# Which engine makes the sums of W_down's blocks, and when: sixteen sets moved between attention, mix, W_o and W_up

## The chip, the cores and the metric

The kernel runs on one core of a Trainium2 chip. The metric is the device time of one execution in microseconds (us). Matmuls run on TensorE (PE), elementwise work on VectorE (DVE), ScalarE (ACT) and GpSimd (POOL); SyncE (SP) issues nearly all transfers.

## The reference

One layer on a stream of 512 tokens by 1024 channels, all in fp32:

```python
h = rms_norm(x, g_pre_mix)
q, k, v, cb, cc, cu, ga, gc = split(h @ w_in)           # 5120 columns
y_attn = stick_breaking_attention(q, k, v) @ w_attn_out  # 8 heads of 64
y_conv = (cb * causal_depthwise_conv(cc * cu, w_conv)) @ w_conv_out
m = sigmoid(ga + b) * y_attn + sigmoid(gc + b) * y_conv
x = x + rms_norm(m @ w_o, g_post_mix)
h = rms_norm(x, g_pre_mlp)
f = square(relu(h @ w_up)) @ w_down                      # 4096 wide
x = x + rms_norm(f, g_post_mlp)
x = x + sigmoid(rms_norm(x, g_ple) @ w_ple_gate) * (p @ w_ple_proj)
```

Stick-breaking attention takes the scores z of a head, `beta = sigmoid(z)` and `keep = sigmoid(-z)`, masks both to the strictly causal part, and multiplies beta by the running product of keep from the right.

## The kernel before

Each fp32 operand of a product is split into a high part (a cast on ACT, line L64, tiles `whi`, `wth`, `oyh`) and the rest (a subtraction on DVE, L65, `wlo`, `wtl`, `oyl`), and each product is three matmuls (L89 to L91, helper `mm3`). Weights come in pieces of 512 KB into `raw` tiles (L70, four buffers) and are split there. The stages follow one another: a head that norms and projects v; attention, four rounds j of two heads each, with the conv branch woven in; mix, eight rounds j (the two output projections, gates, product); W_o; W_up; W_down; the gate at the end.

W_up and W_down are computed by a block scheme that needs sums of blocks of the weights (seven products in place of eight). For W_down the sums are made ahead of time. `make_sums` does one of sixteen sets: it saves the set before it (L279, two transfers of 512 KB from tiles `w` to DRAM, `wsum`), loads two pieces of `w_down` (L290, 512 KB each), and makes four sums of 128x512 (L296) on POOL, or on the engine that it is handed. `save_sums` alone issues the transfers to DRAM. Before, two sets are made ahead of attention and four in it (one a round, all on DVE), eight in mix (one a round, on POOL), and two in W_o (k = 0 and 2, on POOL).

What orders the work: PE and SP run in the order in which the code is written (`manual_schedule`). The others are ordered by a scheduler by priority; `tc.high_priority(-LATE)` puts a block 150 places later in that order. Whatever the order, each engine then runs its instructions one after the other, and one that waits holds up all behind it.

In a round of attention, `scores` makes 1280 columns of beta and keep for a head on ACT (L329, L330). POOL masks them (L335, AFFINE_SELECT of 128x128), and DVE runs the products (L338, a scan, four a head, and L339). The conv branch is on DVE too: L385 multiplies by a projection in a PSUM bank, L388 and L390 make the convolution, L395 multiplies by the last projection and so frees its bank. `wtrans` turns beta over on PE (L354) and splits it; `av` multiplies it by v (L368). `proj_q` and `proj_k` lay out the next round's q and k in `st` (L304, L306; L314, whose high parts ACT casts at L313); PE's scores (L326, L327) read them.

Of the kernel before, what the change touches and what calls it, by code (L numbers as in the profile page):

```python
# [25 lines left out]
LATE = 150  # L26
# [7 lines left out]
def hybrid_block(ctx, tc, x, p, g_pre_mix, w_in, b_gate, w_conv, w_attn_out, w_conv_out, w_o,  # L34
                 g_post_mix, g_pre_mlp, w_up, w_down, g_post_mlp, g_ple, w_ple_gate, w_ple_proj, out):
    nc = tc.nc
# [23 lines left out]
    def tm(dt=F32):  # L60
        return tmp.tile([P, 512], dt, tag="tmp", name="tmp")
# [16 lines left out]
    def w4(dt=F32):  # L78
        return wts.tile([P, 2, 512], dt, tag="w", name="w4")
# [196 lines left out]
    def save_sums():  # L276
        while unsaved:
            dst, src = unsaved.pop(0)
            nc.sync.dma_start(dst, src)  # L279
# [3 lines left out]
    def make_sums(eng=None):  # L283
        eng = eng or nc.gpsimd
        save_sums()
        j = next(made)
        q = []
        for h in range(2):
            t = w4()
            nc.sync.dma_start(t, wd[j][h].rearrange("p (c n) -> p c n", c=2))  # L290
            q += [t[:, 0], t[:, 1]]
        dst = wsum[j // 2][:, :, j % 2, :]
        o = [w4(), w4()]
        t1, t2, t3, t4 = (o[i // 2][:, i % 2] for i in range(4))
        for r, x_, y_ in ((t1, q[1], q[0]), (t2, q[3], t1), (t3, q[3], q[1]), (t4, q[2], t2)):
            eng.tensor_tensor(r, x_, y_, op=ALU.subtract)  # L296
        unsaved.extend([(dst[:, 0:2], o[0]), (dst[:, 2:4], o[1])])
# [95 lines left out]
    def conv_b(c, y):  # L393
        ps = proj(wcols(w_in, 1536 + c * P), hx)
        nc.vector.tensor_tensor(y, ps, y, op=ALU.mult)  # L395
        split(oy_h[1][:, c], oy_l[1][:, c], y)
# [15 lines left out]
    for j in range(4):  # L412
        wa = scores(st[0])
        wb = scores(st[1])
        y = conv_u(j, ct)
        conv_b(j, y)
        ta = wtrans(wa)
        if j < 3:
            st = proj_q(j + 1)
        else:  # L420
            sg[0] = gate(0, 0)
        tb = wtrans(wb)
        if j < 3:
            proj_k(j + 1, st)
        else:
            sg[1] = gate(0, 1)
        of = tm()
        with tc.high_priority(-LATE):
            make_sums(nc.vector)
        av(2 * j, ta, of)  # L430
        av(2 * j + 1, tb, of)
        if j < 3:
            ct = conv_c(j + 1)
# [11 lines left out]
    def oyc(part):  # L445
        return lambda k: (oy_h[part][:, k, :], oy_l[part][:, k, :])

    for j in range(NK):
        make_sums()
        sa, sc = sg if j == 0 else (next_gate if j == 1 else gate(j, 0), gate(j, 1))  # L450

        def two(t, j=j):
            return [(t[:, 4 * i:4 * i + 4], w[:, j * P:(j + 1) * P].rearrange("(k p) m -> p k m", p=P))
                    for i, w in ((1, w_conv_out), (0, w_attn_out))]

        wo2 = weights(two, [P, NK, P])
        save_sums()
        py = proj(wo2, oyc(1), 4, 4)
        nc.vector.tensor_tensor(sc, sc, py, op=ALU.mult)
        if j == 0:  # L460
            next_gate = gate(1, 0)
        py = proj(wo2, oyc(0), 4, 0)
        nc.vector.tensor_tensor(sa, sa, py, op=ALU.mult)
        nc.vector.tensor_tensor(sa, sa, sc, op=ALU.add)
        split(m_h[j // 4][:, j % 4], m_l[j // 4][:, j % 4], sa)
        if j == 3:
            for t in range(NT):
                nc.sync.dma_start(xr[t // 2][:, t % 2, :], x[t * P:(t + 1) * P, :])
        if j == 6:
            nc.sync.dma_start(pf, p[0].rearrange("(t p) d -> p t d", p=P))  # L470
            nc.sync.dma_start(wpr, w_pp.rearrange("(k p) m -> p k m", p=P))
            split(wph, wpl, wpr)
        if j == 7:
            for kk in range(2):
                ps = bank()
                for t in range(NT):
                    nc.tensor.transpose(ps[:, t * P:(t + 1) * P], pf[:, t, kk * P:(kk + 1) * P], ident)
                split(pt[:, kk], pt[:, 2 + kk], ps)


    def rows(nk, stat, w, tail, chain):
        acc = {}
        held = {}
        for k in range(nk):
            if k in (0, 2):
                make_sums()
            if k in (1, 3):
                save_sums()
            wk = wrow(w, k)
            if k >= nk - tail:  # L490
                held[k] = wk
                continue
            sh, sl = stat(k)
            for t in range(NT):
                tok = slice(t * P, (t + 1) * P)
                for hf in range(2):
                    if k == 0:
                        acc[t, hf] = bank()
                    cs = slice(hf * 512, (hf + 1) * 512)
                    mm3(acc[t, hf], sh[:, tok], sl[:, tok], wk[0][:, cs], wk[1][:, cs], k == 0, False)  # L500
        for t in range(NT):
            tok = slice(t * P, (t + 1) * P)
            for hf in range(2):
                cs = slice(hf * 512, (hf + 1) * 512)
                for k in range(nk - tail, nk):
                    sh, sl = stat(k)
                    wk = held[k]
                    mm3(acc[t, hf], sh[:, tok], sl[:, tok], wk[0][:, cs], wk[1][:, cs], False, k == nk - 1)
            chain(t, [acc[t, 0], acc[t, 1]])
# [114 lines left out]
    def up_load(c):  # L624
        r = []
        for h in range(2):
            raw = raws.tile([P, NK, P], F32, tag="raw", name="raw")
            nc.sync.dma_start(raw, w_up[:, (c + h * NJ) * P:(c + h * NJ + 1) * P].rearrange("(k p) m -> p k m", p=P))
            r.append(raw)
        a11, a12, a21, a22 = r[0][:, 0:4], r[0][:, 4:8], r[1][:, 0:4], r[1][:, 4:8]  # L630

        def both(n0, n1, src):
            if c == FIRST or n0 == 6:
                hl = bigt([P, 2, NK, P], name="us")
                hi, lo = hl[:, 0], hl[:, 1]
            else:
                lo, hi = (wts.tile([P, NK, P], F32R, tag="w", name="us") for _ in range(2))
            split(hi, lo, src)
            up_s[c, n0] = hi[:, 0:4], lo[:, 0:4]
            up_s[c, n1] = hi[:, 4:8], lo[:, 4:8]  # L640

        s1 = s1p.tile([P, 4, P], F32, tag="s1", name="s1")
        nc.vector.tensor_tensor(s1, a21, a22, op=ALU.add)
        both(1, 2, r[0])
        nc.vector.tensor_tensor(a11, s1, a11, op=ALU.subtract)
        nc.vector.tensor_tensor(a21, a12, a11, op=ALU.subtract)
        nc.vector.tensor_tensor(a12, a22, a11, op=ALU.subtract)  # L647
        both(6, 7, r[0])
        one_ = wts.tile([P, 2, 4, P], F32R, tag="w", name="us1")
        split(one_[:, 0], one_[:, 1], s1)  # L650
        up_s[c, 5] = one_[:, 0], one_[:, 1]
        both(3, 4, r[1])

    def up_mm(c, n):
        onto = n in (6, 5, 3, 4)
        key = {6: 1, 5: 1, 3: 1, 4: 7}.get(n, n)
        if not onto:
            up_ps[c, n] = bank()
        ps = up_ps[c, key][:, 0:256]
        sh, sl = up_s[c, n]  # L660
        th, tl = rt[n]
        for k in range(4):
            mm3(ps, sh[:, k], sl[:, k], th[:, k], tl[:, k], k == 0 and not onto, k == 3, onto)
        if n == 1:
            ct[c] = [tm(), tm()]
            nc.scalar.copy(ct[c][0][:, 0:256], ps)
        c11, c12, c21, c22 = (ct[c][i // 2][:, 256 * (i % 2):256 * (i % 2) + 256] for i in range(4))
        if n == 2:
            nc.vector.tensor_tensor(c11, ps, c11, op=ALU.add)
        elif n == 6:  # L670
            nc.scalar.copy(c21, ps)
        elif n == 7:
            nc.scalar.copy(c22, ps)
        elif n == 5:
            nc.vector.tensor_tensor(c22, ps, c22, op=ALU.add)
        elif n == 4:
            nc.vector.tensor_tensor(c21, ps, c21, op=ALU.add)
        elif n == 3:
            nc.scalar.copy(c12, ps)
            for h in range(2):  # L680
                nc.scalar.activation(ct[c][h], ct[c][h], AF.Relu)
                nc.scalar.activation(af[c // 4 + 4 * h][:, c % 4], ct[c][h], AF.Square)
            if c % 4 == 3:
                g = c // 4
                nc.vector.tensor_tensor(quarter(1, 0, g), quarter(1, 0, g), quarter(1, 1, g), op=ALU.add)
# [8 lines left out]
    for _, c, n in order:  # L694
        if n == 6 and c + 1 < NJ:
            up_load(c + 1)
        up_mm(c, n)


# [188 lines left out]
```

## Time and profile before

| what | value |
|---|---|
| time, median of three runs | 746.45 us (744.97 to 746.55) |
| the profiled execution's own time | 746.06 us |
| its span in the profile | 744.0 us, so 2.06 us lie around it |
| busy: PE, DVE, ACT, POOL | 730.5, 539.1, 396.2, 108.0 us |
| share of the chain that ended last | PE 82%, DVE 6%, DMA 5%, ACT 3%, POOL 2% |

Times within the profile are us from the start of the span. A timeline row gives the start, the length, and in brackets how long the engine had sat idle before it and what ended that. Rows of the same kind that follow each other closely are merged (x3).

### The profile page before, as it was taken

Reading aid. Unit: us, or ns where it says so; the run is one execution under the profiler, and the core shown is the slowest. Engines: PE = TensorE matmul, PEld = TensorE weight load, DVE = VectorE, ACT = ScalarE, POOL = GpSimd, SP = SyncE. Lnnn points to the kernel's source line nnn. Section 1 sums busy time; section 2 is a strip of 40 time slices with the busy share of each in tenths; the row PEclk is TensorE's granted clock in tenths of the full one; section 3 lists DMA queues with packets and bytes.
Section 4 is the critical chain, followed back from the end, with each engine's and each line's share of the span. In section 5 each row is a group of like instructions: output and inputs, shape, how many; then the busy total and the mean of one; then the engine's idle time right before and its main releaser. Section 6 shows DMA issues by size and latency. Waiting matters only on the chain.

```text
span 744.0 us, 10442 instructions
## 1 busy us (share of the span) xinstructions
PE 730.5 (98%) x3936; PEld 632.4 (85%) x3936; DVE 539.1 (72%) x747; ACT 396.2 (53%) x672; POOL 108.0 (15%) x131
## 2 busy tenths in 40 slices
PE   7999999998999999999999999999999999999997
PEld 6888788887888888878899999999988888888876
DVE  4889898959755424554869879977699878268762
ACT  6555656462533322442855776867776476256531
POOL 0005051347425222200100000000000000001100
PEclk8999999999999999999999999999999999999999
DMA  8393727157599885752244444432555767577311
GB/s 310 126 327 107 221 100 227 54 199 252 178 346 273 254 281 193 269 161 57 106 178 112 115 115 114 118 110 86 168 160 174 224 243 230 174 245 263 128 58 58
DMA packets 112107, 132.30 MB, mean 178 GB/s; under 512 B 4116, under 2 KB 82744, under 8 KB 111032
## 3 DMA queue, kind: packets, MB, share of 16 engines
q1 hardware_dynamic: 111480, 127.44, 53.8%
q10 hardware_dynamic: 576, 4.19, 1.4%
q8 instruction: 31, 0.51, 0.3%
q14 instruction: 20, 0.16, 0.1%
HBM read 108.55 MB, written 23.07 MB: 177 GB/s over the span
## 4 chain that ended last, share of the span: by engine, by line
PE 82%; DVE 6%; DMA 5%; ACT 3%; POOL 2%; issue 1%; SPq 1%; DVEq 0%; POOLq 0%; ACTq 0%
PE ps L89 26%; PE ps L90 26%; PE ps L91 26%; DVE wlo L65 1%; DMA w<-in_w_down_dram 1%; DMA raw<-wsum 1%; PE ps L368 1%; POOL w L296 1%; DMA xin<-in_x_dram 1%; DMA wsum<-w 1%; DMA raw<-in_w_o_dram 1%; ACT whi L64 1%; DVE keep L338 1%; PE ps L354 1%; PE ps L548 1%
## 5 line engine op out<-in xcount | busy, mean ns | idle before, releaser
L65 DVE TENSOR_TENSOR wlo<-raw,whi 128x512 fp32r<-128x512 f32 x120 | 89.4, 776 | 45.8 <-ACT whi L64 19.7
L89 PE MATMUL ps<-h1h,whi 128*128 128x512 f32 x288 | 113.8, 395 | 2.7 <-DVE tmp L395 2.7
L91 PE MATMUL ps<-h1h,wlo 128*128 128x512 f32 x288 | 112.8, 392 | 0.0
L90 PE MATMUL ps<-h1l,whi 128*128 128x512 f32 x288 | 112.7, 391 | 0.0
L64 ACT CAST whi<-raw 128x512 fp32r<-128x512 f32 x120 | 69.1, 638 | 49.6 <-DMA raw<-in_w_in_dram 16.0
L89 PE MATMUL ps<-w,sb 128*128 128x512 f32 x216 | 84.1, 389 | 0.0
L91 PE MATMUL ps<-w,sb 128*128 128x512 f32 x216 | 84.0, 389 | 0.0
L90 PE MATMUL ps<-w,sb 128*128 128x512 f32 x216 | 84.0, 389 | 0.0
L65 DVE TENSOR_TENSOR w<-raw,w 128x1024 fp32r<-128x1024 f32 x56 | 67.7, 1222 | 22.0 <-PE ps L90 11.6
L64 ACT CAST w<-raw 128x1024 fp32r<-128x1024 f32 x56 | 58.4, 1051 | 37.5 <-DMA raw<-wsum 13.4
L125 POOL TENSOR_TENSOR rs<-ms,mhalf 128x1 f32<-128x1 f32 x20 | 14.5, 726 | 409.0 <-DVE ms L121 367.6
L89 PEld LDWEIGHTS ps<-h1h,whi 128*128 128x128 f32 x288 | 54.5, 189 | 13.8 <-DVE tmp L395 2.9
L91 PEld LDWEIGHTS ps<-h1h,wlo 128*128 128x128 f32 x288 | 54.3, 189 | 11.5
L90 PEld LDWEIGHTS ps<-h1l,whi 128*128 128x128 f32 x288 | 54.6, 189 | 11.0
L89 PE MATMUL ps<-h2h,us 128*128 128x256 f32 x224 | 63.5, 283 | 0.0
L90 PE MATMUL ps<-h2l,us 128*128 128x256 f32 x224 | 63.4, 283 | 0.0
L91 PE MATMUL ps<-h2h,us 128*128 128x256 f32 x224 | 63.4, 283 | 0.0
L65 DVE TENSOR_TENSOR us<-raw,us 128x1024 fp32r<-128x1024 f32 x42 | 50.7, 1219 | 7.9 <-ACT us L64 7.7
L64 ACT CAST us<-raw 128x1024 fp32r<-128x1024 f32 x42 | 43.4, 1050 | 19.1 <-DVE raw L647 7.5
L89 PE MATMUL ps<-tb,us 128*128 128x256 f32 x168 | 47.9, 285 | 0.0
L90 PEld LDWEIGHTS ps<-w,sb 128*128 128x128 f32 x216 | 40.5, 188 | 8.5
L89 PEld LDWEIGHTS ps<-w,sb 128*128 128x128 f32 x216 | 40.5, 188 | 8.4
(206 smaller groups left out, 1715.6 us busy)
## 6 DMA issues: line engine op xcount, KB each, us to landing
raw<-in_w_in_dram SPq DMA_DIRECT2D x36, 512.0 KB, 6.9
w<-in_w_down_dram SPq DMA_DIRECT2D x32, 512.0 KB, 4.3
wsum<-w SPq DMA_DIRECT2D x32, 512.0 KB, 3.8
raw<-in_w_up_dram SPq DMA_DIRECT2D x32, 512.0 KB, 4.5
raw<-wsum SPq DMA_DIRECT2D x32, 512.0 KB, 5.1
raw<-in_w_down_dram SPq DMA_DIRECT2D x24, 512.0 KB, 4.3
raw<-in_w_o_dram SPq DMA_DIRECT2D x8, 512.0 KB, 6.0
raw<-in_w_ple_gate_dram SPq DMA_DIRECT2D x8, 512.0 KB, 6.7
```

The source lines that it names most:

```text
L64: nc.scalar.copy(hi, src)
L65: nc.vector.tensor_tensor(lo, src, hi.bitcast(F32), op=ALU.subtract)
L89: nc.tensor.matmul(ps, lh, rh, start=start, stop=False, skip_group_check=onto)
L90: nc.tensor.matmul(ps, lh, rl, start=False, stop=False, skip_group_check=onto)
L91: nc.tensor.matmul(ps, ll, rh, start=False, stop=stop, skip_group_check=onto)
L125: nc.gpsimd.tensor_tensor(r, m, mhalf, op=ALU.pow)
L296: eng.tensor_tensor(r, x_, y_, op=ALU.subtract)
L338: nc.vector.tensor_tensor_scan(kr, kr, kr, 1.0, op0=ALU.mult, op1=ALU.bypass)
L354: nc.tensor.transpose(ps[:, c0 + (qb - kb) * P:c0 + (qb - kb + 1) * P], w[:, o:o + P], ident)
L368: nc.tensor.matmul(ps[:, kb * P:S], lhs, wt[i][:, c0:c0 + n], start=(kb == 0 and i == 0), stop=(kb == NT - 1 and i == 1))
L548: nc.tensor.transpose(ps[:, i * P:(i + 1) * P], hn1[t][g][:, i * P:(i + 1) * P], ident)
```

## The change

The sixteen sets stay; what changes is where each is made and on which engine. Attention makes two (rounds 1 and 2, on DVE) in place of four. Mix makes its first two on DVE at the late priority and the other six on POOL. W_o makes three, one on POOL (k = 0) and two on DVE at the ordinary priority (k = 1 and 3). W_up makes the last, on DVE, at the loads of its sixth chunk (c = 4), and saves it at c = 6. So DVE makes nine sets in place of six, and POOL seven in place of ten. No matmul moves.

```diff
@@ attention, round j
-        with tc.high_priority(-LATE):
-            make_sums(nc.vector)
+        if j in (1, 2):
+            with tc.high_priority(-LATE):
+                make_sums(nc.vector)
         av(2 * j, ta, of)
@@ mix
     for j in range(NK):
-        make_sums()
+        if j > 1:
+            make_sums()
+        else:
+            with tc.high_priority(-LATE):
+                make_sums(nc.vector)
@@ W_o (function rows)
-            if k in (0, 2):
-                make_sums()
-            if k in (1, 3):
+            if k in (0, 1, 3):
+                make_sums(nc.gpsimd if k == 0 else nc.vector)
+            if k == 4:
                 save_sums()
@@ W_up
         if n == 6 and c + 1 < NJ:
             up_load(c + 1)
+            if c == 4:
+                make_sums(nc.vector)
+            if c == 6:
+                save_sums()
```

Because the sets are handed out in turn, the first set of mix in the changed kernel takes about the place that attention's fourth had. Lines below attention carry higher numbers in the changed kernel; the tile numbers (`w_848`) differ too.

DVE before the scores of attention's round 0, kernel before (`wlo` rows are weight splits, `st` rows the layout of q and k, the scan is the first of the round):

```order
L306 TENSOR_TENSOR st<-ps,st 64x512
L65 TENSOR_TENSOR wlo<-raw,whi 128x512 x3
L314 TENSOR_TENSOR st<-ps,st 64x512 x2
L296 TENSOR_TENSOR w_848<-w_844 128x512
L314 TENSOR_TENSOR st<-ps,st 64x512
L296 TENSOR_TENSOR w_848<-w_846,w_848 128x512
L314 TENSOR_TENSOR st<-ps,st 64x512
L296 TENSOR_TENSOR w_849<-w_846,w_844 128x512
L296 TENSOR_TENSOR w_849<-w_846,w_848 128x512
L338 SCALAR_TENSOR_TENSOR keep<-keep 128x512
```

The same place in the changed kernel:

```order
L306 TENSOR_TENSOR st<-ps,st 64x512
L65 TENSOR_TENSOR wlo<-raw,whi 128x512 x5
L314 TENSOR_TENSOR st<-ps,st 64x512 x3
L65 TENSOR_TENSOR wlo<-raw,whi 128x512
L314 TENSOR_TENSOR st<-ps,st 64x512
L65 TENSOR_TENSOR wlo<-raw,whi 128x512
L338 SCALAR_TENSOR_TENSOR keep<-keep 128x512
```

Four sums are gone, and the splits of two further weight pieces stand there instead, two splits of them ahead of all the `st` of k.

POOL around the masks of attention's round 3, kernel before (`w_1955` is mix's first set, `w_2042` its second):

```order
L296 TENSOR_TENSOR w_1955<-w_1951 128x512
L296 TENSOR_TENSOR w_1955<-w_1953,w_1955 128x512
L296 TENSOR_TENSOR w_1956<-w_1953,w_1951 128x512
L296 TENSOR_TENSOR w_1956<-w_1953,w_1955 128x512
L335 AFFINE_SELECT beta<-beta 128x128
L335 AFFINE_SELECT keep<-keep 128x128
```

POOL after the last masks of that round in the changed kernel (`w_2105` is mix's third set):

```order
L335 AFFINE_SELECT beta<-beta 128x128
L335 AFFINE_SELECT keep<-keep 128x128
L296 TENSOR_TENSOR w_2105<-w_2101 128x512
L296 TENSOR_TENSOR w_2105<-w_2103,w_2105 128x512
L296 TENSOR_TENSOR w_2106<-w_2103,w_2101 128x512
```

No sum stands ahead of round 3's masks any more; the first that follows them is mix's third set.

DVE in round 3, from the last `st` of k to the first scan, kernel before:

```order
L65 TENSOR_TENSOR oyl<-tmp,oyh 128x512
L314 TENSOR_TENSOR st<-ps,st 64x512
L338 SCALAR_TENSOR_TENSOR keep<-keep 128x512
L339 TENSOR_TENSOR beta<-beta,keep 128x511
```

The same place in the changed kernel, and further on, from L385 to L395 (`w_2018` and `w_2019` are mix's second set):

```order
L314 TENSOR_TENSOR st<-ps,st 64x512
L65 TENSOR_TENSOR wlo<-raw,whi 128x512 x2
L296 TENSOR_TENSOR w_2018<-w_2014 128x512
L338 SCALAR_TENSOR_TENSOR keep<-keep 128x512
...
L385 TENSOR_TENSOR tmp<-tmp,ps 128x512
L296 TENSOR_TENSOR w_2018<-w_2016,w_2018 128x512
L388 TENSOR_SCALAR tmp<-tmp,cols 128x512
L296 TENSOR_TENSOR w_2019<-w_2016,w_2014 128x512
L390 SCALAR_TENSOR_TENSOR tmp<-tmp,cols 128x511
L65 TENSOR_TENSOR wlo<-raw,whi 128x512
L390 SCALAR_TENSOR_TENSOR tmp<-tmp,cols 128x510
L296 TENSOR_TENSOR w_2019<-w_2016,w_2018 128x512
L395 TENSOR_TENSOR tmp<-ps,tmp 128x512
```

One sum, which needs the load of `w_2014`, now stands ahead of round 3's first scan, and three stand among the steps of the convolution.

## Rows read from the trace of the kernel before

**Rows 1.** Waits of PE: us in total, times, longest.

```profile
PE ps L89 <- DVE tmp L395: 2.7, 1, 2.7
...
PE ps L368 <- DVE wtl L65: 0.3, 1, 0.3
PE ps L327 <- DVE st L314: 0.3, 1, 0.3
PE ps L89 <- DVE pt L65: 0.2, 1, 0.2
```

**Rows 2.** Timeline of PE, second turning of beta in attention's round 1.

```profile
111.74 1.25 PE L354 MATMUL ps<-ident,beta 128*128 128x128 f32 x10
112.75 0.48 PE L89 MATMUL ps<-h1h,whi 128*128 128x512 f32 x1
```

**Rows 3.** Timeline of PE, the same step of round 3.

```profile
180.93 1.25 PE L354 MATMUL ps<-ident,beta 128*128 128x128 f32 x10
184.88 0.80 PE L89 MATMUL ps<-h1h,whi 128*128 128x512 f32 x1 [2.71 <-DVE tmp L395]
...
187.98 0.39 PE L90 MATMUL ps<-h1l,whi 128*128 128x512 f32 x1
```

**Rows 4.** Windows: length, engines' busy us, then PEclk, DMA share, GB/s.

```profile
185.00:190.00 5.00, 5.00 (x16) 4.05 (x17) 4.91 (x7) 5.00 (x12) 3.96 (x3) 0.71 0.98 302
```

**Rows 5.** Timeline of POOL in round 3.

```profile
161.03 3.79 POOL L296 TENSOR_TENSOR w<-w,w 128x512 f32<-128x512 f32 x3
...
175.67 4.89 POOL L296 TENSOR_TENSOR w<-w,w 128x512 f32<-128x512 f32 x3
```

**Rows 6.** Timeline of DVE in round 3.

```profile
165.35 1.29 DVE L338 TENSOR_TENSOR_SCAN keep<-keep 128x512 f32<-128x512 f32 x1 [6.21 <-POOL keep L335]
...
177.91 1.50 DVE L339 TENSOR_TENSOR beta<-beta,keep 128x255 f32<-128x255 f32 x1
...
184.14 0.69 DVE L395 TENSOR_TENSOR tmp<-ps,tmp 128x512 f32<-128x512 f32 x1
```

**Rows 7.** Timeline of DVE in round 2, the same steps.

```profile
128.49 1.23 DVE L338 TENSOR_TENSOR_SCAN keep<-keep 128x512 f32<-128x512 f32 x1 [0.92 <-POOL keep L335]
...
139.10 0.41 DVE L339 TENSOR_TENSOR beta<-beta,keep 128x255 f32<-128x255 f32 x1
...
144.27 0.68 DVE L395 TENSOR_TENSOR tmp<-ps,tmp 128x512 f32<-128x512 f32 x1
```

**Rows 8.** Timeline of ACT at the start of round 3.

```profile
161.74 0.62 ACT L64 CAST whi<-raw 128x512 fp32r<-128x512 f32 x1 [3.46 <-DMA raw<-in_w_conv_out_dram]
...
163.35 0.61 ACT L330 ACTIVATE keep<-ps 128x512 f32<-128x512 f32 x1
```

**Rows 9.** The chain that ended last: start, us, what; attention's round 0.

```profile
71.08 5.84 DMA wsum<-w
...
76.97 3.73 DMA w<-in_w_down_dram
...
94.42 0.23 PE ps L89
```

**Rows 10.** Timeline of DVE in round 0.

```profile
80.79 0.69 DVE L296 TENSOR_TENSOR w<-w 128x512 f32<-128x512 f32 x1 [1.52 <-DMA w<-in_w_down_dram]
```

**Rows 11.** Timeline of ACT ahead of round 0's scores.

```profile
44.85 0.62 ACT L64 CAST whi<-raw 128x512 fp32r<-128x512 f32 x1 [0.67 <-DMA raw<-in_w_in_dram]
...
46.66 0.62 ACT L64 CAST whi<-raw 128x512 fp32r<-128x512 f32 x1 [0.18 <-DMA raw<-in_w_in_dram]
```

**Rows 12.** Timeline of PE, second head's scores in round 0.

```profile
56.93 0.40 PE L327 MATMUL ps<-st 128*128 128x512 f32 x1
```

**Rows 13.** Loads of `raw` (line L70) from 36 to 60 us.

```profile
DMA to landing us min/median/max: 5.0/7.0/9.1
```

**Rows 14.** Loads of the blocks of W_down (line L290), the whole span.

```profile
DMA to landing us min/median/max: 3.2/4.3/7.9
```

**Rows 15.** Windows, a stretch of W_up (columns as in rows 4).

```profile
400.00:450.00 50.00, 50.00 (x416) 49.81 (x415) 43.59 (x61) 34.98 (x60) 0.00 (x0) 1.00 0.45 127
```

## The prediction

> **What bounds the kernel now.** I read the waits of PE first, since PE is busy in nearly the whole span: only work that PE waits for, or that slows its clock, can change the time. Outside the head and the tail four waits are left, 2.7, 0.3, 0.3 and 0.2 us [rows 1], so nearly all that any rearrangement of sums can win is one place, the wait on L395 in round 3 of attention. The timeline of PE gives that place its whole price. In round 1 the same step takes 112.75 - 111.74 = 1.01 us from the turning of beta to the next projection [rows 2]; in round 3 it takes 184.88 - 180.93 = 3.95 us [rows 3], so 2.94 us are lost. Behind it the clock is down: the windows show a granted clock of 0.71 from 185 to 190 us [rows 4], a stretch partly at the lower of the two levels, 1.2 GHz in place of 2.4, after PE had stood still for 2.7 us. The seven steps from 184.88 to 187.98 take 3.10 us [rows 3]; at the 0.23 us of an undisturbed one [rows 9] they take 1.61, so 1.5 us more are lost. Price of the place: 2.94 + 1.5 = 4.4 us.
>
> Next, why L395 is late. The timelines of POOL and DVE, read side by side, show two causes. POOL makes mix's first set ahead of the masks: its last three sums run from 161.03 to 164.82 [rows 5], and only then come the masks, on which DVE's first scan waits: DVE has sat idle for 6.21 us when it starts at 165.35 [rows 6], though ACT's first keep was done at 163.96 [rows 8]. ACT adds to it: ahead of round 3's beta and keep stands a weight split that waited 3.46 us for a load of W_conv_out and ran at 161.74 [rows 8]; without it the two activations would run about 1.2 us sooner (the split's 0.62 us, and as much again since it began late). Then DVE itself is slower: from first scan to L395 it takes 144.27 - 128.49 = 15.78 us in round 2 [rows 7] and 184.14 - 165.35 = 18.79 us in round 3 [rows 6]. The 3.0 us more lie where POOL's next sums run, from 175.67 on [rows 5]: one beta product of 128x255 takes 1.50 us beside them [rows 6] and 0.41 us without [rows 7].
>
> In round 0 the chain that ended last runs over the sums too: the save of the set before (landed at 76.92), then the load of the next (from 76.97, 3.73 us) [rows 9], for which DVE waited 1.52 us [rows 10] with all of its later work queued behind; the waits for `wtl` and `st` (0.34 and 0.30 us by rows 1, rounded there) come right after it.
>
> **The change, part by part.** The sums cost the same everywhere: two loads, two saves, four sums. So each part is asked only whether it moves a wait of PE.
>
> *Round 3.* POOL has no sum left ahead of the masks, and none until they are done. Also, W_conv_out's load is issued earlier, since one set's transfers fewer stand ahead of it. With POOL's share of the delay gone (165.35 - 163.96, less some 0.3 us for the one mask between: 1.1 us) and ACT's 1.2 us as well, the first scan starts at about 165.35 - 2.3 = 163.1. From there I take round 2's 15.78 us: in both orders five fillers (splits there, splits and sums here, about 0.6 to 0.7 us each) stand among L385 to L395. So L395 starts at 178.9 and ends at 179.6. PE needs it at 184.88 - 2.71 = 182.2. It is no longer late, by 2.6 us, and the 4.4 us go. Bounds: if only POOL's slowing of DVE goes and the scan stays at 165.35, L395 ends at 181.8, still in time; if something new holds DVE for more than the 2.6 us, part comes back (rivals). What is late next: nothing on DVE that PE needs here, since the turned weights queue behind L395 in the same order.
>
> *Round 0, gain.* Its set is gone, so the load for round 1's set no longer waits for a save of it. The save ahead of it is that of a set made before attention, so the load can go out as soon as the raw loads ahead of it are out: by about 70 us, when SP issued the saves before. With the median landing of 4.3 us [rows 14] it is there at 74.5, with the slowest of 7.9 at 78; DVE needs it at 79.3, when it began to wait (80.79 - 1.52). The 1.52 us of waiting go. PE gets back at least its two waits, 0.64 us, and at most 1.5 us; I take 1.1, since the matmuls beside these waits were late too.
>
> *Round 0, cost.* Two splits of a further weight piece now stand ahead of k's `st` on ACT and DVE, and two of a second piece among them. Their loads are the next two behind four that were in flight. Landings there are 46.66 - 44.85 = 1.8 us apart [rows 11], so after those at 46.6 and 48.4 they land near 50.2 and 52.0. From ACT's cast at 52.0 on I count two splits (0.6 each) and the last two rounds of `st`, each a cast and a subtraction in turn (1.3): the last `st` is ready at 57.2, and PE reads it at 56.93 [rows 12]. Cost 0.3 us. Bounds: nothing if one lands 0.3 us sooner; at the slowest landing of this stretch, 9.1 us against the 5.0 that I assume for the first [rows 13], 4.1 us more and up to 1.5 us of clock.
>
> *Mix.* Its first two sets leave POOL, and POOL's remaining six have the same distance from PE as before; no wait of PE stands in mix [rows 1]. Nothing.
>
> *W_o.* POOL slows DVE no more in its later part, and DVE's eight sums (5.5 us) lie in idle time while it waits for loads. The wait for `pt`, 0.2 us, goes. Bounds 0.2 gained to 0.2 more lost; I take -0.2.
>
> *W_up.* Four sums, 2.4 us, on an engine that is busy 43.59 of 50 us [rows 15]. The free 6.4 us in 50 take them up within about 20 us; PE shows no idle time in this stretch. Cover gone, it costs 2.4 us and the clock behind it, 1.5. I take nothing.
>
> Sum: -4.4 - 1.1 + 0.3 - 0.2 = -5.4 us. What the waits do not show (a split of `wtl` in round 3 that POOL's sums slow as well, behind 190 us) may give some tenths more; I take -5.8. Against the profiled execution's 746.06 us this is 740.3. That execution was 0.4 us faster than the median of the three runs, 746.45; a median of new runs may lie as much higher.
>
> **A rule of the skill against the move.** In the row above, POOL's sum of 1.29 us beside it made a product of DVE 1.1 us longer. The Trainium skill (SBUF — State Buffer, "Who interferes with whom") says that a DVE instruction with two SBUF inputs and a GpSimd instruction that reads SBUF exclude each other, and that whichever starts first keeps the other out for its whole length. By that rule the move works in both directions: the sum that now stands on DVE ahead of round 3's first scan can hold back a mask on POOL for as long as it runs. That would delay the scan by up to 0.7 us, the slack of 2.6 us would be 1.9, and the sum would stay -5.8; it makes the second rival below a little likelier.
>
> **The rivals.** A difference below 0.2% (1.5 us) is one that a measurement of this kernel cannot tell from none.
>
> *First, the wait moves to round 0's `st`.* For: ACT takes the new splits in order, so a late landing holds k's casts behind it, with no slack. Against: the queue is emptier than before, without two loads and two saves. If the second load lands 2 to 4 us later than 52.0, PE waits that long, with 1.5 us of clock: 740.3 + 2 to 5.5, so 742.3 to 745.8.
>
> *Second, DVE is held by a load in round 3.* The first sum of mix's second set stands ahead of the first scan, and needs `w_2014`, whose buffer and issue wait for the save of the set before. By the old order's times the issue comes at about 158.3; with 3.2 to 4.3 us it lands at 161.5 to 162.6, before the scan at 163.1; with 7.9 [rows 14] at 166.2, so 3.1 us late against 2.6 of slack. Then PE waits 0.5 us or, with the rule above, 1.2; with a later issue more. 741 to 744.5.
>
> *Third, W_up's cover is missing.* 740.3 + 2.4 + 1.5 = 744.2.
>
> *Fourth, no effect.* The wait on L395 has another cause (for: ACT's share was a load; against: the 3 us between the rounds' lengths fit POOL's sums). Then 745 to 746.5.
>
> *Slower.* The second rival in the large: everything on DVE behind `w_2014` waits, and PE stands. It costs 1 us for each beyond the slack and gives the clock's 1.5 back as loss. All 5.8 us are eaten if the load comes 2.6 + 5.8 - 1.5 = 6.9 us after 163.1, at 170.0 or later, 11.7 us after issue; the time is then over 746.1, and 748 at 172. The slowest landing of its kind took 7.9 us.
>
> **How the numbers follow.** Forecast 0.62; first rival 0.13, second 0.09, third 0.05, fourth 0.06, slower 0.05. The predicted time is the forecast's, 740.3. Its own range is 738.6 (all 1.5 us in round 0, no cost there, some tenths of the later splits) to 741.8 (round 0 gives nothing and costs 0.3). The range for 8 in 10 takes in most of the first three rivals: 738.4 to 744.8. Faster by over 0.2% (below 744.95) are the forecast and the first three but for their upper ends: 0.84; within 0.2%: 0.11; slower 0.05.
>
> **What would show it.** In the waits of PE, L395 is gone, and from 180 to 190 us the granted clock is at 1.00. POOL's first mask of round 3 follows ACT's beta at once, and the scan to L395 takes about 16 us. In round 0 DVE does not wait for W_down's load. Wrong would be a new wait of PE on `st` near 57 us, an idle DVE ahead of round 3's first scan that W_down's load ends, or waits of PE on `us` or on DVE's additions between 420 and 450 us.

## The result and the profile after

The changed kernel took 738.19 us (median of four runs, 736.68 to 738.59) against 746.07 us of the kernel before in the same rounds (four runs, 744.97 to 746.55): a ratio of 0.9893, interval 0.9874 to 0.9911. The forecast was 740.3, range 738.4 to 744.8: the way was right, and the time lies 0.2 us below the range. Timed again over more runs (below), the two kernels stand at 738.48 us (6 runs) and 744.5 us (17 runs), ratio 0.9926, interval 0.9898 to 0.9953 (a ratio over all runs, not of the two medians).

The page of the profile after, span and busy us:

```profile
span 736.3 us, 10436 instructions
PE 726.8 (99%) x3936; PEld 630.8 (86%) x3936; DVE 537.7 (73%) x759; ACT 398.2 (54%) x672; POOL 89.1 (12%) x119
```

All waits of PE after (us in total, times, longest):

```profile
PE ps L175 <- POOL ident masks.py:199: 1.4, 1, 1.4
PE ps L89 <- ACT vh L64: 1.2, 1, 1.2
PE ps L89 <- DVE tmp L680: 1.2, 2, 0.7
PE ps L90 <- DVE vl L65: 0.5, 1, 0.5
PE ps L89 <- ACT tmp L671: 0.5, 1, 0.5
PE ps L90 <- DVE wlo L65: 0.2, 1, 0.2
```

The four waits of [rows 1] are gone. Two others have come: on L680 and L671, the steps of W_up that empty PSUM banks. The waits on `vh` and `vl` lie in the head, which the change does not touch. Round 3 of attention, DVE's timeline and then PE's:

```profile
157.35 0.69 DVE L296 TENSOR_TENSOR w<-w 128x512 f32<-128x512 f32 x1
158.93 1.23 DVE L338 TENSOR_TENSOR_SCAN keep<-keep 128x512 f32<-128x512 f32 x1 [0.90 <-POOL keep L335]
...
174.82 0.68 DVE L395 TENSOR_TENSOR tmp<-ps,tmp 128x512 f32<-128x512 f32 x1
```

```profile
176.72 1.25 PE L354 MATMUL ps<-ident,beta 128*128 128x128 f32 x10
177.73 0.48 PE L89 MATMUL ps<-h1h,whi 128*128 128x512 f32 x1
```

From the scan to L395 it is 15.89 us (15.78 were forecast, 18.79 before [rows 6]), and L395 ends 2.2 us ahead of PE's next projection, which follows the turning after 1.01 us as in [rows 2]. The scan's start, 158.93, is 4.17 us earlier than the forecast's 163.1. Nearly as much earlier everything runs here: the turning of beta in round 1, at 111.74 before, stands at 107.53.

The next table has the length of each stage of PE's timeline, from profiles of this study: head (to the first score matmul, L326 before), attention (to the first matmul with `oyh` and `whi`), mix to the start of W_up (to the first matmul with `us`), W_up (to the last such), rest (to the end of the span).

| kernel | head | attention | mix, W_o | W_up | rest | span |
|---|---|---|---|---|---|---|
| before | 55.44 | 139.55 | 202.12 | 141.63 | 205.26 | 744.0 |
| before, second profile | 51.50 | 139.29 | 203.09 | 141.28 | 205.84 | 741.0 |
| after | 52.74 | 133.02 | 201.62 | 144.02 | 204.90 | 736.3 |
| after, second profile | 54.21 | 133.06 | 201.62 | 143.38 | 204.63 | 736.9 |

Attention gave 6.2 to 6.5 us, mix and W_o 0.5 to 1.5, and W_up lost 1.8 to 2.7. The head differs by 3.9 us between two profiles of one and the same kernel.

### The profile page after: what moved, and what is told of

The parts are those of the page before. It is cut to its first block, busy times and chain, and to the rows that moved or that the text cites. A ratio compares the mean times of both kernels' runs of the same rounds, so it can differ in the third digit from the quotient of the medians.

```text
span 736.3 us, 10436 instructions
## 1 busy us (share of the span) xinstructions
PE 726.8 (99%) x3936; PEld 630.8 (86%) x3936; DVE 537.7 (73%) x759; ACT 398.2 (54%) x672; POOL 89.1 (12%) x119
## 4 chain that ended last, share of the span: by engine, by line
PE 87%; DVE 6%; DMA 4%; issue 1%; ACT 1%; POOL 0%; SPq 0%; ACTq 0%; DVEq 0%; POOLq 0%
PE ps L90 27%; PE ps L89 27%; PE ps L91 27%; DMA raw<-in_w_up_dram 2%; DVE us L65 2%; PE ps L368 1%; PE ps L354 1%; DMA raw<-wsum 1%; PE ps L327 1%; PE ps L326 1%; ACT junk L117 1%; DMA xin<-in_x_dram 1%; PE ps L553 1%; PE ps L194 0%; DVE x L519 0%
## 5 line engine op out<-in xcount | busy, mean ns | idle before, releaser
L65 DVE TENSOR_TENSOR wlo<-raw,whi 128x512 fp32r<-128x512 f32 x120 | 83.8, 729 | 45.5 <-ACT whi L64 21.4
```

What stands on the lines that cost most here:

```text
L65: nc.vector.tensor_tensor(lo, src, hi.bitcast(F32), op=ALU.subtract)
```

## The experiments

**The same kernel again.** No edit.

> The kernel before, unchanged, for a second profile. In the two profiles so far the head differs by 2.5 to 2.8 us though its work is the same: ACT starts on the second piece of x at 7.98 us before and at 6.28 after. If that is a matter of chance in one execution, this profile can show either, and times of the kernel before spread as widely; if it belongs to the changed kernel, this one shows 8.0 again.

It took 742.95 us, in rounds whose runs of the kernel before went from 740.44 to 745.88 (median 744.06 of 15). ACT in the head, in this profile:

```profile
4.15 1.06 ACT L117 ACTIVATE junk<-xin 128x1024 bf16<-128x1024 f32 x1 [1.86 <-DMA xin<-in_x_dram]
...
6.16 1.06 ACT L117 ACTIVATE junk<-xin 128x1024 bf16<-128x1024 f32 x1 [0.85 <-DMA xin<-in_x_dram]
```

The second piece of x was there at 6.16 us. In the first profile of this kernel it came later:

```profile
7.98 1.06 ACT L117 ACTIVATE junk<-xin 128x1024 bf16<-128x1024 f32 x1 [2.65 <-DMA xin<-in_x_dram]
```

The granted clock differed in the head too. From 10 to 20 us it was 0.66 in the first profile and 1.00 in the second (columns as in rows 4):

```profile
10.00:20.00 10.00, 8.80 (x30) 7.04 (x31) 9.18 (x25) 8.62 (x25) 0.55 (x1) 0.66 0.91 329
10.00:20.00 10.00, 9.87 (x49) 8.01 (x50) 9.66 (x28) 9.02 (x25) 0.56 (x2) 1.00 0.86 315
```

So the head is a matter of chance in an execution, and the 746.06 us that the prediction subtracted from held a long one.

**The changed kernel again,** timed against the kernel before over more runs.

> The changed kernel, unchanged, timed against the kernel before in the same rounds. The head of the kernel before took 4 us less in its second profile than in its first, with the wait of PE on vh 1.5 us in place of 2.2 and on vl 0.2 in place of 1.1, so the head is a matter of chance in each execution. If the changed kernel wins only by its own places (5.0 in round 3, 1.4 in round 0, 0.5 in W_o, less 2.4 in W_up: 4.5 us, and up to 0.6 at the tail), the ratio over many runs is 0.993 to 0.994; if the head belongs to it, 0.989 again.

738.48 us against 744.5, ratio 0.9926 (0.9898 to 0.9953): just under the first theory's 0.993 to 0.994, with the interval holding it, and 0.9893 outside. In its profile the second piece of x came at 7.95, in the first profile of the changed kernel at 6.28. The head does not belong to the change.

**Only the engine of mix's first two sets,** in the kernel before:

```diff
-        make_sums()
+        if j > 1:
+            make_sums()
+        else:
+            with tc.high_priority(-LATE):
+                make_sums(nc.vector)
```

> The kernel before, with one edit: the first two sets of mix are made on DVE at the late priority; attention keeps its four sets, W_o its two. Theory (POOL's sums ahead of the masks and beside DVE's products are the whole cause of the stall in round 3): the wait on L395 goes, 4.4 to 5.0 us, so about 741.4 against 746.1 (ratio 0.994). Rival (the stall goes because attention's fourth set went, not because POOL was freed): the wait stays, or a wait for the moved sums takes its place, and the time is within 1.5 us of 746.1.

738.34 us against 744.06, ratio 0.9925 (0.9905 to 0.9945). Attention takes 134.02 us, 5.3 to 5.5 less than before, the wait on L395 is gone, and W_up has its 141.28. From the second turning of beta in round 3 to the end of attention PE takes 9.04 us, as in the changed kernel; before it took 14.07 and 14.16 us in the two profiles. One edit of the change's five does what all five do together. Attention's set of round 3 need not go.

**The first of these two sets alone, and the second alone,** both in the kernel before (`j == 0`, or `j == 1`, on DVE; the rest on POOL).

> The kernel before; only mix's first set goes to DVE (late priority), the second stays on POOL. This takes away POOL's sums ahead of round 3's masks and leaves those beside DVE's products. If the late masks are the larger cause (2.2 us of the first scan's start), L395 is late by 0.4 us or less, and most of the 5 us of round 3 are won. If the slowed products alone suffice (3.0 us), a wait of 2 us or more on L395 stays.

> The kernel before; only mix's second set goes to DVE, the first stays on POOL ahead of the masks. By the prediction's bound the scan then starts at 165.35 as before and L395 ends about 0.4 us before PE needs it, so the wait goes all the same. If the late masks alone suffice for the stall, a wait of 2 us or more stays.

The first alone: 744.51 us against 744.48, ratio 1.000 (0.9977 to 1.0022), a wait on L395 of 1.6 us left, which lies between the two outcomes expected. The second alone: 740.1 us, ratio 0.995 (0.9931 to 0.9969), no wait on L395. DVE with the first set moved, the masks in time, POOL's second set beside:

```profile
161.58 1.23 DVE L338 TENSOR_TENSOR_SCAN keep<-keep 128x512 f32<-128x512 f32 x1 [1.67 <-POOL keep L335]
...
172.71 1.71 DVE L65 TENSOR_TENSOR wlo<-raw,whi 128x512 fp32r<-128x512 f32 x1
174.34 1.50 DVE L339 TENSOR_TENSOR beta<-beta,keep 128x255 f32<-128x255 f32 x1
...
180.57 0.69 DVE L395 TENSOR_TENSOR tmp<-ps,tmp 128x512 f32<-128x512 f32 x1
```

And with the second set moved, the masks late, POOL idle at that place:

```profile
162.49 1.29 DVE L338 TENSOR_TENSOR_SCAN keep<-keep 128x512 f32<-128x512 f32 x1 [6.10 <-POOL keep L335]
...
172.33 0.66 DVE L65 TENSOR_TENSOR wlo<-raw,whi 128x512 fp32r<-128x512 f32 x1
172.91 0.41 DVE L339 TENSOR_TENSOR beta<-beta,keep 128x255 f32<-128x255 f32 x1
...
177.68 0.69 DVE L395 TENSOR_TENSOR tmp<-ps,tmp 128x512 f32<-128x512 f32 x1
```

The two scans start 0.9 us apart, but L395 follows after 18.99 us in the one and 15.19 in the other, though DVE runs the same instructions in between. The split and the product shown, two products of 128x383 ahead of them (1.88 us together against 0.78) and the split behind L385 (1.07 against 0.69) make 3.6 of these 3.8 us. The slowed instructions are the deciding cause; the late masks only add to them. Attention takes 138.79 us with the first set moved, 0.5 to 0.8 less than before, and 134.30 with the second, 5.0 to 5.2 less. With the first, PE also waited 1.55 us for a `wtl` further on, as it did in the second profile of the kernel before (1.54). Both lost in mix and W_o, which took 204.58 and 206.01 us, with waits on `pt` (0.8 us in both) and, in the second, on mix's product at L467 (0.8 us); that loss was not followed up.

**One part undone:** the changed kernel with mix's first two sets on POOL (the diff above, reversed).

> The changed kernel with one part undone: the first two sets of mix are on POOL again; attention keeps two sets, W_o three, W_up one. Theory (POOL's sums ahead of the masks and beside DVE make the stall of round 3): the wait on L395 is there again, 2 to 3 us, and the time is 3 to 5 us above the changed kernel's. Rival (attention's fewer sets take the stall away as well): no wait on L395, and the time is the changed kernel's within 1 us.

741.95 us against the changed kernel's 738.48 in the same rounds, 3.5 more (ratio to before 0.9968, 0.9949 to 0.9988). The wait on L395 is back, with 1.8 us, and attention takes 136.88. What is left of the gain, 2.4 to 2.7 us of attention, comes from the sets that left it.

**Only round 0's set gone,** to W_o (k = 4, POOL), in the kernel before:

```diff
-        with tc.high_priority(-LATE):
-            make_sums(nc.vector)
+        if j > 0:
+            with tc.high_priority(-LATE):
+                make_sums(nc.vector)
...
-            if k in (0, 2):
+            if k in (0, 2, 4):
                 make_sums()
-            if k in (1, 3):
+            if k in (1, 3, 5):
                 save_sums()
```

> The kernel before; only attention's set of round 0 goes, to W_o (k = 4, on POOL). By the changed kernel's trace round 0 then gives 1.4 us net (1.7 won, 0.3 lost at the scores), with no wait of PE on wtl or st of round 0, and the wait on L395 stays; W_o may take some of it back, as a third set there did once (2 to 3 us at the residual). Rival: round 0's wait has another cause and stays.

742.75 us, ratio 0.9979 (0.9962 to 0.9996). The waits on round 0's `wtl` and `st` are gone, the wait on L395 stays (2.7 us), attention takes 138.45, so 0.8 to 1.1 us less. Up to round 3's second turning of beta, ahead of the stall, 1.1 to 1.5 us are won. W_o took nothing back (201.87).

**W_up's set, put elsewhere or changed.** Five variants of the changed kernel. First, the set made in W_o in its place:

```diff
-            if k in (0, 1, 3):
-                make_sums(nc.gpsimd if k == 0 else nc.vector)
+            if k in (0, 1, 2, 3):
+                make_sums(nc.gpsimd if k in (0, 2) else nc.vector)
...
-            if c == 4:
-                make_sums(nc.vector)
-            if c == 6:
-                save_sums()
```

> The changed kernel, but the set of W_up is made in W_o at k = 2 on POOL in its place. Theory (W_up's set costs DVE 2.4 us that its free time there does not take up, since that time is spent waiting for loads): the three new waits of PE in W_up, 1.7 us in the waits and 2.2 us with the slower steps beside them, are gone, and the time falls from 738.2 to about 735.9. Rival (the waits in W_up come from another cause, such as a different phase of the loads): they stay, and the time stays within 0.5 us of 738.2.

740.1 us (10 runs) against 744.06, ratio 0.9942 (0.9921 to 0.9963). W_up went back to 141.28, but mix and W_o took 205.05 in place of 201.62, so the 735.9 expected did not come. PE's timeline at the place:

```profile
357.17 0.39 PE L91 MATMUL ps<-wph,pt 128*128 128x512 f32 x1
359.51 1.40 PE L553 MATMUL ps<-ident,tmp 128*128 128x128 f32 x8 [1.95 <-DVE tmp L536]
...
361.13 0.63 PE L90 MATMUL ps<-wpl,pt 128*128 128x512 f32 x1
361.56 0.63 PE L91 MATMUL ps<-wph,pt 128*128 128x512 f32 x1
```

and the window behind it (columns as in rows 4):

```profile
361.00:366.00 5.00, 5.00 (x17) 3.93 (x17) 4.12 (x8) 3.49 (x8) 0.18 (x2) 0.70 0.64 221
```

PE waited for the residual, and ran on at a granted clock of 0.70. The waits in W_up did come from the set; where it went, it cost more in this profile (3.4 us of the stage).

Second, the set on POOL instead of DVE (`make_sums(nc.gpsimd)` at c = 4), and third, its sums left out, with only loads and saves:

> The changed kernel with W_up's set on POOL instead of DVE; its loads, saves and buffers stay where they are. If DVE's 2.4 us are the cause of the waits in W_up, most of them go, less what POOL's four sums take from DVE by the side (up to 1.1 us each by the rows of round 3): 736 to 737.5. If the buffers or the transfers of the set are the cause, the waits stay and the time is 738.2 or more.

> The changed kernel, but W_up's set leaves out its four sums: it makes its two loads and two saves, of the loaded blocks as they are, so the last set's values are not the sums. If DVE's 2.4 us alone make PE's waits in W_up, all three waits (1.7 us) are gone. If the set's transfers or its tiles are part of it, some stay; with the sums on POOL 1.1 us of waits stayed, which by the first theory is what POOL's sums take from DVE.

Fourth, the sums on DVE two and two (`wup_spread`: the four are issued one a chunk, c = 4 to 7, which the scheduler puts into two pairs, and the save comes at c = 9):

> The changed kernel with W_up's four sums on DVE apart: two at the place of before, two some 25 us later, the saves three chunks later. If DVE's free time in W_up takes up 1.2 us but not 2.4 at one time, the waits of PE between 440 and 500 us (1.2 to 2.2 us with the steps beside them in the two profiles of the changed kernel) fall under 0.7 us. If a backlog of DVE does not drain there at all, since DVE's free time is spent waiting for loads that go out later when DVE is late, the waits stay at 1 us or more.

| W_up's set | W_up, us | DVE busy in it, us | time, us (ratio to before, interval) |
|---|---|---|---|
| none | 141.28 | 116.2 | 740.1 (0.9942, 0.9921 to 0.9963), W_o longer |
| loads and saves only | 142.10 | 116.3 | 737.52, one run |
| sums on DVE, two and two | 142.55 | 118.7 | 739.23 (0.9938, 0.9924 to 0.9953) |
| sums on POOL | 143.17 | 119.5 | 738.0 (0.9922, 0.9899 to 0.9944) |
| sums on DVE (the changed kernel) | 144.02, 143.38 | 118.4, 118.5 | 738.48 (0.9926, 0.9898 to 0.9953) |

The loads and saves alone cost 0.8 us, the sums on DVE at one place 1.3 to 1.9 more, two and two 0.45 more; the last is less than the 0.6 by which two profiles of the changed kernel differ. Sums on POOL cost 1.1 more, nearly as much as on DVE: DVE's own instructions then took 3.2 us longer, where the sums on DVE itself add 2.2. Of the waits on DVE and ACT, 1.5 to 1.7 us in the changed kernel, 0.3 us were left without the sums, 0.7 with the pairs, and 1.1 with POOL. So the sums are most of the cause and not the whole. The loss does not follow DVE's busy time: the pairs add as much of it as the four sums at one place and cost less.

The pairs' losses, with the steps beside the waits, are 1.0 us, on the expected side of a backlog that does not drain. But by the same count 0.5 us are lost without any sums, so this measure could not tell the two theories apart. The times of these kernels cannot tell the variants apart; the stage can, with one profile each.

What the set does without its sums shows in DVE's order. In the kernel before (second profile) the first step on a newly loaded piece begins as soon as the load has landed, 21.9 us after the start of W_up:

```profile
415.80 0.69 DVE L643 TENSOR_TENSOR s<-raw 128x512 f32<-128x512 f32 x1 [0.29 <-DMA raw<-in_w_up_dram]
```

With loads and saves only, the same step comes 31.1 us after the start of W_up. Its load had landed at 22.0, but it now stands behind steps that wait for ACT and PE, and DVE idles ahead of them:

```profile
414.74 1.23 DVE L695 TENSOR_TENSOR af<-af 128x1024 f32<-128x1024 f32 x1 [2.12 <-ACT af L692]
417.40 0.42 DVE L685 TENSOR_TENSOR tmp<-ps,tmp 128x256 f32<-128x256 f32 x1 [1.43 <-PE ps L91]
...
419.21 0.68 DVE L653 TENSOR_TENSOR s<-raw 128x512 f32<-128x512 f32 x1
```

In the changed kernel the step comes at 31.4, in the same order. The set thus also put DVE's other work in another order. That the 0.8 us come from this was not tried by itself.

Fifth, the set as a second one on POOL in round 4 of mix:

```diff
+        if j == 4:
+            make_sums()
         if j == 3:
             for t in range(NT):
                 nc.sync.dma_start(xr[t // 2][:, t % 2, :], x[t * P:(t + 1) * P, :])
...
-            if c == 4:
-                make_sums(nc.vector)
-            if c == 6:
-                save_sums()
```

> The changed kernel, but the set of W_up is made in mix instead, as a second set on POOL in round 4. Theory (W_up's set is what makes PE wait in W_up, and mix has no wait of PE for POOL's sums): W_up's waits go, nothing takes their place, and the time is 2 to 2.4 us below that of the changed kernel in the same rounds. Rival (as in W_o, where a second set on POOL moved the wait to the residual): a new wait in mix or W_o takes the gain, and the time is within 0.7 us of the changed kernel's.

736.47 us against 738.48 of the changed kernel in the same rounds; ratio to before 0.9891 (0.9867 to 0.9916). All waits of PE in its profile:

```profile
PE ps L89 <- ACT vh L64: 2.0, 1, 2.0
PE ps L175 <- POOL ident masks.py:199: 1.4, 1, 1.4
PE ps L90 <- DVE vl L65: 1.1, 1, 1.1
PE ps L90 <- DVE wlo L65: 0.6, 1, 0.6
```

Between the head and the last stage none is left, W_up takes 141.30 and mix and W_o 201.61. The two intervals overlap, but the stage lengths say where the 2 us are. This is the fastest of the kernels tried.

## Why the prediction missed, step by step

**The base failed.** "Against the profiled execution's 746.06 us this is 740.3" took one execution's head for the kernel's. In the fourteen profiles of this study the head ends between 51.50 and 55.44 us, at 53.7 in the mean; 746.06 was at the long end. Against the 744.5 of 17 runs the same -5.8 gives 738.7, beside a measured 738.48; the ratio of those rounds, 0.9926, is a gain of 0.74%, and 5.8 of 746.06 is 0.78%. The range did not allow for a base 1.6 us lower, and "a median of new runs may lie as much higher" looked to the wrong side. The four runs of the kernel before in the first rounds were all as long (744.97 and more); of the 68 in later rounds 20 were. Only one of the four was profiled, so what made the other three long stays open.

**That the sum of -5.8 agrees is luck.** By the table, in the means of the two profiles each, attention gave 6.4 us where the terms for it, with the "some tenths", make 5.6; mix and W_o gave 1.0 for 0.2; the rest 0.8 for nothing, which is within its spread (below); and W_up took 2.2 for nothing. Three gains too small and one cost left out cancel to within 0.2 us.

**W_up, taken at nothing, cost 1.8 to 2.7 us.** This is the third rival, with its place and without its clock: the granted clock stayed at 1.00 there. The failed step is "the free 6.4 us in 50 take them up within about 20 us". The three losses of PE in the first profile come some 30 to 80 us after the sums. DVE's free time lay ahead of loads: of the 6.4 us free in the stretch of [rows 15], it waited 5.2 for loads of W_up. 22 us after the last sum DVE still waits there, though it is behind, and then PE loses at the end of a chunk:

```profile
438.74 0.69 DVE L648 TENSOR_TENSOR s<-raw 128x512 f32<-128x512 f32 x1 [2.23 <-DMA raw<-in_w_up_dram]
```

```profile
461.67 0.28 PE L91 MATMUL ps<-tb,us 128*128 128x256 f32 x1
462.68 0.39 PE L89 MATMUL ps<-h2h,us 128*128 128x256 f32 x1 [0.73 <-DVE tmp L680]
```

That step of DVE comes 51.36 us after the start of W_up, against 49.40 and 48.22 in the two profiles of the kernel before. Its load went out later as well, at 45.36 against 43.28 and 43.43. That a late split holds back the next load's issue, so that the wait and the backlog go on together, fits these rows; it was not tried by itself. The pairs speak against its being all, since they add as much work and cost 0.45 us, and so does the changed order of DVE.

**Round 3 was right on its wait, and wrong on what lay behind it.** 4.4 us and "some tenths" were forecast. From round 3's second turning to the end of attention the one edit gave 5.0 to 5.1 us (the rest of its 5.3 to 5.5 lies ahead of that turning, where the two profiles of the kernel before differ by 0.35 themselves). The clock's 1.5 us in the forecast's price were those of one execution. In the second profile of the kernel before PE stood still as long, the granted clock from 180 to 190 us stayed at 1.00, and PE waited for `wtl` behind it:

```profile
180.68 0.50 PE L89 MATMUL ps<-h1h,whi 128*128 128x512 f32 x1 [2.80 <-DVE tmp L395]
...
189.47 0.50 PE L368 MATMUL ps<-wtl,v 128*128 128x512 f32 x1 [1.54 <-DVE wtl L65]
```

```profile
180.00:185.00 5.00, 4.32 (x19) 3.57 (x20) 4.91 (x7) 4.34 (x9) 2.83 (x3) 1.00 1.07 341
```

The loss was the same. In the first profile, too, PE's last products begin right after the `wtl` that they read (at 193.67 and 194.26, after 193.62 and 194.21), so DVE set the end in both, and the lower clock only filled a wait. DVE was late there by the delay of L395, and because POOL's next set slowed four splits; the first row is from the kernel before, the second from the one with mix's second set moved, POOL idle:

```profile
187.05 5.96 DVE L65 TENSOR_TENSOR wlo<-raw,whi 128x512 fp32r<-128x512 f32 x4
```

```profile
182.81 2.50 DVE L65 TENSOR_TENSOR wlo<-raw,whi 128x512 fp32r<-128x512 f32 x4
```

So 2.9 to 3.0 of the 5.0 to 5.1 us are the stop at L395, as forecast; the other 2 us are DVE's delay at `wtl`, where the forecast had a clock of 1.5 and "some tenths". Every time of the walk held, once shifted by the 4.2 us: the scan, the 15.8 us, L395 with over 2 us of slack. The order of the causes did not. The prediction put the start (2.2 us) and the slowed products (3.0) side by side, and its own bound, that L395 is in time even with a scan at 165.35, proved to be the main thing.

**Round 0 was right.** -1.1 + 0.3 were forecast; round 0's set alone gave 0.8 to 1.1 us of attention, and 1.1 to 1.5 up to the stall in round 3. The cost's sum does not come out as written: 52.0, two splits of 0.6 and two rounds of 1.3 make 55.8, not 57.2. The last `st` was done at 54.24 us by DVE's timeline, 56.94 with the longer head of the profile before; PE, which would have read it at 54.23, lost 0.2 us there:

```profile
54.00 0.39 PE L326 MATMUL ps<-st 128*128 128x512 f32 x1
54.30 0.50 PE L327 MATMUL ps<-st 128*128 128x512 f32 x1
54.63 0.34 PE L326 MATMUL ps<-st 128*128 128x384 f32 x1
```

**W_o**, with mix, gave 0.5 to 1.5 us in place of 0.2; the wait for `pt`, 0.2 us in the first profile, was 0.8 in the second. **The rest** varied between 204.4 and 205.8 us whatever the change.

**The first two rivals did not come.** DVE made the first sum of mix's second set without waiting for its load (157.35 in the rows above), and the scan waited only for POOL's mask, 0.90 us as in [rows 7]. The rule of the Trainium skill (SBUF — State Buffer, "Who interferes with whom"), that a DVE instruction with two SBUF inputs and a GpSimd instruction reading SBUF keep each other out, agrees in direction with the two rows for `wlo`, 1.71 and 0.66 us, in the experiments on mix's first and second set. The sums of POOL beside the slowed product in the kernel before took 1.47 to 1.76 us, not the 1.29 that the prediction names. The price forecast for the first mask of round 3 hardly came to be tried: ACT's beta was done at 158.00, the sum on DVE at 158.04, and the mask began at 158.06. But a DVE instruction does hold a mask back in these rows. Two masks took 0.3 us, and the third, which began 0.11 us after DVE's scan of 1.23 us (158.93 above), took 1.21 and ended 0.09 us after it:

```profile
158.06 0.30 POOL L335 TENSOR_SCALAR_AFFINE_SELECT beta<-beta 128x128 f32<-128x128 f32 x1 [24.89 <-DVE w L296]
158.60 0.29 POOL L335 TENSOR_SCALAR_AFFINE_SELECT keep<-keep 128x128 f32<-128x128 f32 x1 [0.24 <-PE ps L327]
159.04 1.21 POOL L335 TENSOR_SCALAR_AFFINE_SELECT beta<-beta 128x128 f32<-128x128 f32 x1
```

## What to carry to other kernels

Before a predicted gain is subtracted from a profiled execution, look at how far the stages that the change does not touch vary between executions; with a second profile, compare stage by stage. Free time counted over a stretch does not say that new work fits in: look at what ends the idle time, how much work comes at one place, and whether the new work changes the order of the engine's other work. A clock that fell behind one wait in one execution is not a price of that wait: see whether another execution shows it. When two causes share a wait, move each alone: here the one that showed as 6 us of idle time was worth under 1 us by itself.

## What was not expected of the hardware

The landing of the second piece of x in the head differed by 1.8 us between executions of one kernel (7.98 and 6.16), the granted clock from 10 to 20 us was 0.66 in one and 1.00 in the other, and the head as a whole differed by 3.9 us. After PE had stood still for 2.71 us in round 3 the granted clock from 185 to 190 us was 0.71; in another execution of the same kernel it stayed at 1.00 after 2.80 us. Four sums on POOL beside W_up, 128x512 each, lengthened the stage by 1.1 us more than the loads and saves alone and DVE's own instructions by 3.2 us; the pairs on DVE lengthened the stage by 0.45 us.
